# A hybrid decoder step on one core: the delta rule's triangular inverse with its small block products split into shorter groups

## The chip, the cores and the metric

One core of a Trainium2 chip. The metric is the device time of one execution in microseconds. The matrix engine is PE in the profile (PEld is its weight load), VectorE is DVE, ScalarE is ACT, GpSimd is POOL, SyncE is SP.

## The reference

The kernel computes one inference step of a two-layer decoder trunk for a prompt of 1024 tokens and 8 samples of one token. Layer 0 mixes retention and sparse attention, layer 1 is a gated DeltaNet with 8 heads of width 128; each has a squared-ReLU MLP. What the change touches is the delta rule of layer 1, computed in chunks:

```python
m = jnp.where(strict, jnp.einsum('nbhid,nbhjd->nbhij', kb, kc) * gam, 0.0)
eye = jnp.eye(chunk, dtype=f32)
t_inv = lax.linalg.triangular_solve(eye + m, jnp.broadcast_to(eye, m.shape), left_side=True, lower=True)
u = jnp.einsum('nbhij,nbhje->nbhie', t_inv, vc * bc[..., None])
w = jnp.einsum('nbhij,nbhjd->nbhid', t_inv, kb * jnp.exp(gc)[..., None])
```

## The kernel before

Layer 1 (`odd`, from L1632) goes head by head. The kernel uses chunks of 128, so each of the 8 heads has 8 chunks, and for each a triangular matrix of 128 x 128 is inverted. `inverse_blocks` (L2022) inverts the 16 x 16 blocks on the vector engine; `inverse_rest` (L2055) puts them together with small products on the matrix engine, for all 8 chunks of a head at once: 32 x 32 blocks from 16 x 16 ones (L2065, two sets of 32 products), 64 x 64 blocks from 32 x 32 ones (L2083, L2093, L2096), 128 x 128 from 64 x 64 (L2106, L2111). The products address a 32 x 32 or 64 x 64 part of the array.

All this is woven into the dense projections. `mm3` (L181) does three matmuls per k-step and then calls `tick` (L232), which takes one step of one of two lanes in turn; when the lane whose turn it is has nothing left, the other is taken. A step is what a generator does up to its next `yield`. Lane 0 holds `head(h)` (decays, products of keys and queries, `inverse_blocks`), lane 1 holds `chain(h - 1)`: first `inverse_rest`, then the recurrence over the 8 chunks (L1840 to L1871), then the output norm and its transposes (L1833). A head's three projections are 72 k-steps. `chain` takes 34 turns, `head` 14, and `head` does not begin `inverse_blocks` until the chain of the previous head has finished `inverse_rest` (the flag `inv`, which both share tiles for). After the last head the gate projections (L1916 on, 24 k-steps for each of 8 heads) go on with the last two chains in lane 1 and the samples in lane 0; at head 6 of these, what is left of the last chain is drawn in one go (L1915).

The order in which an engine gets its instructions is set at build time by a planner: it goes by the order in the program, raised priorities, and what it reckons to be ready. All PSUM tiles of the lanes (`iv`, `tn`, `m`, `t2`) come from one ring of four banks.

Of the kernel before, what the change touches and what calls it, by code (L numbers as in the profile page):

```python
# [20 lines left out]
OP = mybir.AluOpType  # L21
# [112 lines left out]
class _Step:  # L134
# [1920 lines left out]
    def inverse_rest(self, N, U, Up, Tp, NM, Pt, Pt2, TT):  # L2055

        nc = self.nc
        V = nc.vector
        f = lambda y: y.rearrange("p a b -> p (a b)")
        ps = [self.side('iv'), self.side('iv')]  # L2060
        for p, l, r in ((ps[0], NM, Tp), (ps[1], Pt, Up)):
            for q in range(4):
                x = slice(32 * q, 32 * q + 32)
                for c in range(8):
                    nc.tensor.matmul(p[x, 32 * c:32 * c + 32], l[x, c], r[x, c], start=True, stop=True)  # L2065
            if p is ps[0]:
                nc.scalar.copy(f(Pt), p[:, 0:256])
                yield
        V.tensor_tensor(f(Up), f(Up), ps[1][:, 0:256], op=OP.subtract)
        V.transpose(f(Tp), f(Up))  # L2070
        for q in range(2):
            x = slice(32 * q, 32 * q + 32)
            nc.scalar.copy(TT[x, :, x], Tp[x])
        for q in range(3, -1, -1):
            x = slice(32 * q, 32 * q + 32)
            nc.gpsimd.tensor_copy(U[x, :, x], Up[x])
        yield
        p = self.side('iv')
        v32 = lambda y: y[:, 0:256].rearrange("p (c m) -> p c m", c=8)
        for i in (0, 2):  # L2080
            x, y = slice(32 * i, 32 * i + 32), slice(32 * i + 32, 32 * i + 64)
            for c in range(8):
                nc.tensor.matmul(p[y, 32 * c:32 * c + 32], N[x, c, y], Tp[x, c], start=True, stop=True)  # L2083
        for i in (0, 2):
            y = slice(32 * i + 32, 32 * i + 64)
            with self.tc.high_priority(offset=100):
                nc.scalar.copy(Pt[y], v32(p)[y])
        yield
        p = self.side('iv')
        for i in (0, 2):  # L2090
            x, y = slice(32 * i, 32 * i + 32), slice(32 * i + 32, 32 * i + 64)
            for c in range(8):
                nc.tensor.matmul(p[x, 32 * c:32 * c + 32], Pt[y, c], Up[y, c], start=True, stop=True)  # L2093
        x, y = slice(0, 32), slice(32, 64)
        for c in range(8):
            nc.tensor.matmul(p[y, 32 * c:32 * c + 32], Up[y, c], Pt[y, c], start=True, stop=True)  # L2096
        for i in (0, 2):
            x, y = slice(32 * i, 32 * i + 32), slice(32 * i + 32, 32 * i + 64)
            nc.scalar.mul(U[x, :, y], v32(p)[x], -1.0)
        nc.scalar.mul(TT[32:64, :, 0:32], v32(p)[32:64], -1.0)  # L2100
        yield
        p = self.side('iv')
        lo, hi = slice(0, 64), slice(64, 128)
        v64 = lambda y: y.rearrange("p (c m) -> p c m", c=8)
        for c in range(8):
            nc.tensor.matmul(p[hi, 64 * c:64 * c + 64], N[lo, c, hi], TT[:, c], start=True, stop=True)  # L2106
        nc.scalar.copy(Pt2[hi], v64(p)[hi])
        yield
        p = self.side('iv')
        for c in range(8):  # L2110
            nc.tensor.matmul(p[lo, 64 * c:64 * c + 64], Pt2[hi, c], U[hi, c, hi], start=True, stop=True)  # L2111
        nc.scalar.mul(U[lo, :, hi], v64(p)[lo], -1.0)
        yield
# [117 lines left out]
```

## Time and profile before

| | us |
|---|---|
| timed runs: 2976.19, 2978.12, 2978.9; median | 2978.12 |
| profiled execution | 2991.83 |
| its span, first to last instruction | 2990.2 |
| PE busy in the span | 2878.2 (96%) |
| DVE busy | 1966.3 (66%) |
| ACT busy | 1245.8 (42%) |
| POOL busy | 240.8 (8%) |
| mean granted PE clock | 0.981 |

The steps below are read from the profiled execution, which took 13.7 us longer than the median of the timed runs. A granted clock of 1.00 is 2.4 GHz, 0.50 is 1.2 GHz. PE is the engine to watch: it is busy nearly all the time, though a busy PE can still run at the lower clock.

### The profile page before, as it was taken

The page shows a single profiled execution, that of the slowest core. Times are in us where ns is not written, and L with a number is a line of the kernel's source. Part 1 is how long each engine was busy: PE and PEld are TensorE (multiplying, and loading weights), DVE is VectorE, ACT ScalarE, POOL GpSimd, SP SyncE. Part 2 cuts the span into 40 slices and gives each one's busy share as a digit, 9 for nine tenths or more (in the row PEclk, how much of TensorE's full clock was granted, in tenths as well). Part 3 has the DMA queues.
Part 4 walks back from the last instruction along what each step waited for, and adds up shares of the span by engine and source line. Part 5 has one row for each costly group of instructions (what it writes and reads, how often), then busy time and mean ns, then how long its engine had stood idle before and what let it go on. Part 6 is the DMA issues. An engine that isn't in the chain of part 4 may idle for free. (4 is left out here: it accounts for less than half of the span.)

```text
span 2990.2 us, 57153 instructions
## 1 busy us (share of the span) xinstructions
PE 2878.2 (96%) x22980; PEld 2684.1 (90%) x22980; DVE 1966.3 (66%) x5147; ACT 1245.8 (42%) x2498; POOL 240.8 (8%) x328
## 2 busy tenths in 40 slices
PE   8999999999899999999999999999999999999997
PEld 6559997799799999999988999999998999999997
DVE  4569897448755765454677766764768657765557
ACT  4457734426733431111364565542348434321111
POOL 0210002100000000000001111111100000000002
PEclk9989998999999999999999999998999999999998
DMA  8665325213433556552221222223524426343222
GB/s 277 189 201 142 86 72 177 78 50 106 155 121 128 194 168 191 170 164 94 62 83 40 65 62 49 60 77 113 170 82 129 158 96 205 124 141 106 72 71 65
DMA packets 282678, 358.50 MB, mean 120 GB/s; under 512 B 49494, under 2 KB 230523, under 8 KB 281644
## 3 DMA queue, kind: packets, MB, share of 16 engines
q1 hardware_dynamic: 258786, 272.86, 30.3%
q0 software_dynamic: 23296, 81.85, 8.4%
q8 instruction: 180, 2.95, 0.4%
q14 instruction: 86, 0.70, 0.1%
q10 hardware_dynamic: 330, 0.13, 0.0%
HBM read 271.45 MB, written 80.12 MB: 118 GB/s over the span
## 5 line engine op out<-in xcount | busy, mean ns | idle before, releaser
L188 PE MATMUL bank<-XH,whi 128*128 128x256 f32 (+4 forms) x3488 | 906.3, 305 | 1.9 <-ACT N L1268 0.8
L188 PE MATMUL bank<-XH,wlo 128*128 128x384 f32 (+5 forms) x2720 | 825.5, 304 | 0.9 <-DVE wlo L177 0.9
L188 PE MATMUL bank<-XL,whi 128*128 128x256 f32 (+5 forms) x2976 | 792.6, 302 | 2.2 <-DVE XL L426 1.9
L188 PEld LDWEIGHTS bank<-XH,whi 128*128 128x128 f32 (+1 forms) x3488 | 604.2, 188 | 24.2 <-issue 11.1
L188 PEld LDWEIGHTS bank<-XL,whi 128*128 128x128 f32 (+1 forms) x2976 | 525.7, 188 | 17.8 <-issue 9.5
L188 PEld LDWEIGHTS bank<-XH,wlo 128*128 128x128 f32 (+2 forms) x2720 | 511.7, 188 | 7.8 <-issue 5.0
L638 DVE SCALAR_TENSOR_TENSOR N<-bank,G,N 128x256 f32<-128x256 f32 x576 | 274.8, 481 | 312.6 <-PE bank L188 311.5
L176 ACT CAST whi<-raw 128x1024 fp32r<-128x1024 f32 x142 | 147.5, 1039 | 443.2 <-PE bank L188 397.8
L188 PE MATMUL bank<-W,whi 128*128 128x260 f32 (+1 forms) x1152 | 207.7, 282 | 2.9 <-DVE accS L646 1.5
L177 DVE TENSOR_TENSOR wlo<-raw,whi 128x1024 fp32r<-128x1024 f32 x142 | 173.2, 1220 | 45.6 <-ACT whi L176 44.8
L704 PE MATMUL bank<-W,whi 128*128 128x256 f32 x1094 | 182.9, 284 | 12.4 <-ACT whi L697 7.3
L704 PE MATMUL bank<-W,wlo 128*128 128x256 f32 x1082 | 182.0, 284 | 9.5 <-ACT wlo L697 4.2
L704 PE MATMUL bank<-XH,whi 128*128 128x260 f32 x896 | 181.2, 285 | 8.1 <-ACT N L719 3.0
L704 PE MATMUL bank<-XH,wlo 128*128 128x260 f32 x896 | 181.2, 285 | 4.4 <-DVE wlo L691 3.0
L188 PEld LDWEIGHTS bank<-W,whi 128*128 128x128 f32 x1152 | 176.0, 188 | 8.3 <-DVE N L638 2.5
L697 ACT CAST whi<-raw 128x512 fp32r<-128x512 f32 x168 | 103.9, 622 | 170.9 <-PE bank L704 60.3
L704 PEld LDWEIGHTS bank<-W,whi 128*128 128x128 f32 x1094 | 155.0, 188 | 18.8 <-ACT whi L697 9.5
L704 PEld LDWEIGHTS bank<-W,wlo 128*128 128x128 f32 x1082 | 154.5, 188 | 14.6 <-ACT wlo L697 5.7
L188 PE MATMUL bank<-W,wlo 128*128 128x256 f32 (+1 forms) x576 | 162.0, 283 | 0.5 <-DVE wlo L177 0.5
L691 DVE TENSOR_TENSOR whi<-raw,whi 128x512 fp32r<-128x512 f32 x168 | 115.1, 688 | 67.4 <-ACT whi L697 63.6
L697 ACT CAST wlo<-raw 128x512 fp32r<-128x512 f32 x168 | 103.3, 621 | 133.8 <-PE bank L704 50.4
L691 DVE TENSOR_TENSOR wlo<-raw,wlo 128x512 fp32r<-128x512 f32 x168 | 114.6, 687 | 63.0 <-ACT wlo L697 60.5
(628 smaller groups left out, 5461.0 us busy)
## 6 DMA issues: line engine op xcount, KB each, us to landing
raw<-in_mlp_up_dram SPq DMA_DIRECT2D x96, 512.0 KB, 4.2
N<-in_ada_w_dram SPq DMA_DIRECT2D x80, 512.0 KB, 5.3
W<-hD SPq DMA_DIRECT2D x64, 516.0 KB, 4.4
raw<-in_mlp_down_dram SPq DMA_DIRECT2D x60, 512.0 KB, 3.5
hD<-N POOLq DMA_DIRECT2D x32, 520.0 KB, 4.0
N<-resD SPq DMA_DIRECT2D x32, 512.0 KB, 4.6
hD<-N POOLq DMA_DIRECT2D x32, 512.0 KB, 3.6
raw<-in_odd_w_in_dram SPq DMA_DIRECT2D x32, 512.0 KB, 4.2
```

What stands on the lines that cost most here:

```text
L176: nc.scalar.copy(hi[:, :k * m], raw[:, :k * m])
L177: nc.vector.tensor_tensor(lo[:, :k * m], raw[:, :k * m], hi[:, :k * m], op=OP.subtract)
L188: self.nc.tensor.matmul(out, ww[:, i, ms], xx[:, c0:c1], start=start and i == 0 and j == 0, stop=stop and i == nk - 1 and j == 2)
L638: nc.vector.scalar_tensor_tensor(r, ps[:, :256], g[:, dt, 0:1], r, op0=OP.mult, op1=OP.add)
L691: sub = lambda o, x, y: V.tensor_tensor(o, x, y, op=OP.subtract)
L697: nc.scalar.copy(hi, a)
L704: nc.tensor.matmul(o, ww[:, k], xx, start=start and k == 0 and n == 0, stop=k == 3 and n == 2, skip_group_check=True)
```

## The change

Each set of products in `inverse_rest` is interrupted by a `yield` once part of it is issued: after two of the four strips of 32 partitions in L2065's two sets (16 products, then 16), after the first of the two blocks in L2083's set (8, then 8), and after the first of the blocks in L2093's set (8, then 8 with the 8 of L2096 behind them). The second PSUM tile of L2065's sets is taken when its set begins, not with the first. No operation is added or removed.

```diff
-        ps = [self.side('iv'), self.side('iv')]
-        for p, l, r in ((ps[0], NM, Tp), (ps[1], Pt, Up)):
+        for l, r in ((NM, Tp), (Pt, Up)):
+            p = self.side('iv')
             for q in range(4):
                 x = slice(32 * q, 32 * q + 32)
                 for c in range(8):
                     nc.tensor.matmul(p[x, 32 * c:32 * c + 32], l[x, c], r[x, c], start=True, stop=True)
-            if p is ps[0]:
+                if q == 1:
+                    yield
+            if l is NM:
                 nc.scalar.copy(f(Pt), p[:, 0:256])
                 yield
-        V.tensor_tensor(f(Up), f(Up), ps[1][:, 0:256], op=OP.subtract)
+        V.tensor_tensor(f(Up), f(Up), p[:, 0:256], op=OP.subtract)
...
                 nc.tensor.matmul(p[y, 32 * c:32 * c + 32], N[x, c, y], Tp[x, c], start=True, stop=True)
+            if i == 0:
+                yield
...
                 nc.tensor.matmul(p[x, 32 * c:32 * c + 32], Pt[y, c], Up[y, c], start=True, stop=True)
+            if i == 0:
+                yield
```

## Rows read from the trace of the kernel before

**Rows 1.** The page, section 1: busy us, share of the span, instructions.
```profile
PE 2878.2 (96%) x22980; PEld 2684.1 (90%) x22980; DVE 1966.3 (66%) x5147; ACT 1245.8 (42%) x2498; POOL 240.8 (8%) x328
```
**Rows 2.** Windows: stretch, length, busy us by engine, PE clock, DMA share, GB/s.
```profile
core 0: us, PE busy (x) PEld busy (x) DVE busy (x) ACT busy (x) POOL busy (x), PEclk, DMA share, GB/s
1600.00:2060.00 460.00, 452.32 (x4409) 421.24 (x4408) 298.03 (x1087) 240.00 (x635) 76.25 (x92) 0.96 0.26 68
1609.00:1612.45 3.45, 3.45 (x22) 3.29 (x20) 2.68 (x4) 1.31 (x3) 2.13 (x3) 0.51 0.34 84
1720.00:1740.00 20.00, 20.00 (x317) 18.66 (x317) 11.31 (x28) 13.07 (x33) 4.05 (x5) 1.00 0.18 55
1970.80:1981.10 10.30, 10.30 (x122) 9.54 (x118) 5.30 (x7) 4.72 (x15) 2.42 (x4) 0.50 0.13 52
2034.80:2039.10 4.30, 4.30 (x126) 4.08 (x125) 0.00 (x0) 1.06 (x2) 0.54 (x1) 1.00 0.32 126
2039.10:2059.60 20.50, 20.50 (x152) 18.39 (x151) 3.06 (x6) 5.99 (x13) 4.84 (x7) 0.50 0.41 129
```
**Rows 3.** The product lines, all heads: count, ns min/median/max, first and last start.
```profile
L2065 PE MATMUL bank<-N x1024: 191/191/258, 1604.8 to 2039.0; 32*32 32x32 f32 x171
L2083 PE MATMUL bank<-N,N x256: 191/191/258, 1614.3 to 2042.8; 32*32 32x32 f32 x128
L2093 PE MATMUL bank<-N x256: 191/191/258, 1616.3 to 2046.4; 32*32 32x32 f32 x128
L2096 PE MATMUL bank<-N x128: 191/191/257, 1617.1 to 2047.0; 32*32 32x32 f32 x128
```
**Rows 4.** Timeline of PE (start, us, line, count): a group of 64.
```profile
1719.74 0.33 PE L188 MATMUL bank<-XH,wlo 128*128 128x384 f32 x1
1720.00 1.91 PE L2065 MATMUL bank<-N 32*32 32x32 f32 x64
1721.84 0.44 PE L188 MATMUL bank<-XH,whi 128*128 128x384 f32 x1
1722.12 0.34 PE L188 MATMUL bank<-XL,whi 128*128 128x384 f32 x1
```
**Rows 5.** The same: a group of 32.
```profile
1728.72 0.34 PE L188 MATMUL bank<-XH,wlo 128*128 128x384 f32 x1
1728.99 1.09 PE L2083 MATMUL bank<-N,N 32*32 32x32 f32 x32
1730.01 0.45 PE L188 MATMUL bank<-XH,whi 128*128 128x384 f32 x1
1730.30 0.34 PE L188 MATMUL bank<-XL,whi 128*128 128x384 f32 x1
```
**Rows 6.** The same: a group of 48.
```profile
1731.52 0.33 PE L188 MATMUL bank<-XH,wlo 128*128 128x384 f32 x1
1731.78 1.00 PE L2093 MATMUL bank<-N 32*32 32x32 f32 x29
...
1732.71 0.57 PE L2096 MATMUL bank<-N 32*32 32x32 f32 x13
1733.21 0.44 PE L188 MATMUL bank<-XH,whi 128*128 128x384 f32 x1
1733.49 0.34 PE L188 MATMUL bank<-XL,whi 128*128 128x384 f32 x1
```
**Rows 7.** Timeline of PE ahead of the seventh head's inverse; in brackets idle time before.
```profile
1968.94 0.66 PE L1833 MATMUL bank<-cst,N 128*128 128x128 f32 x4 [1.53 <-DVE N L1827]
...
1969.88 0.81 PE L2065 MATMUL bank<-N 32*32 32x32 f32 x23
```
**Rows 8.** L2053 in two heads, and the second head's first products.
```profile
L2053 DVE STREAM_TRANSPOSE N<-N x2: 436/436/437, 1654.1 to 1711.4; 128x256 f32<-128x256 f32 x2
...
1655.62 0.62 PE L2065 MATMUL bank<-N 32*32 32x32 f32 x14
```
**Rows 9.** Waits of PE, 1600 to 2060: total us, times, longest.
```profile
PE bank L1833 <- DVE N L1827: 4.3, 6, 1.5
```
**Rows 10.** Timeline of PE in the gate projections: the last transposes.
```profile
2120.91 0.60 PE L1833 MATMUL bank<-cst,N 128*128 128x128 f32 x4
```

## The prediction

> **What bounds the kernel now.** I read the page's busy shares first, then the stage in which the change lies, then single groups of products, and last the waits. The matrix engine is busy 96% of the span [rows 1]. In the stretch that holds the eight inverses it is busy 452.32 of 460 us, at a mean granted clock of 0.96 [rows 2]. So the matrix engine sets this stage's end, and the rest of the inverse (copies, vector transposes) runs beside it. What is put on that engine, or what its clock gives back, comes out at the end nearly one for one.
>
> The reader is to see two things in the stage. First, the clock. In three stretches it is granted at 0.50 (1.2 GHz instead of 2.4): 3.45 us in the first head's inverse, 10.30 us in the seventh's, 20.50 us in the eighth's, together 34.25 us [rows 2]. In the other five inverses it stayed at 1.00, as in the third head's stretch [rows 2]. Before the longest fall the engine was not idle: 4.30 of 4.30 us busy, with 126 matmul records, all but a few of them 32x32 products [rows 2]. Second, the products themselves. Per head L2065 has 128 instructions in two runs of 64, L2083 has 32, and L2093 with L2096 has 48 (each product is two instructions) [rows 3].
>
> **What a group of products costs.** One group's whole cost is read from the dense matmuls around it: from the start of the last one before the group to the start of the second one after it, less two ordinary slots. A slot is 1.22/7 = 0.174 us (the seven steps from 1730.30 to 1731.52) [rows 5, 6]. The group of 64: 1722.12 - 1719.74 - 0.35 = 2.03 us [rows 4]. The group of 32: 1730.30 - 1728.72 - 0.35 = 1.23 us [rows 5]. The group of 48: 1733.49 - 1731.52 - 0.35 = 1.62 us [rows 6]. The three lie on a line: 16 instructions more cost 0.40 us, and 0.42 us is left that does not depend on the number. It is spent at the two edges, where the array goes from full tiles to 32x32 tiles and back: the first dense matmul after a group holds its successor for 0.28 us instead of 0.174.
>
> **The change part by part.** Removed: nothing. All products, copies and subtractions stay. Added: four yields per head, which split the two runs of 64 into 32 + 32 each, the run of 32 into 16 + 16 and the run of 48 into 16 + 32. That is 4 x 8 = 32 more groups. Between the halves one turn of the other lane and two k-steps of dense matmuls (six of them) are emitted, so the edges are paid again: 32 x 0.41 = **+13.1 us**. The ends of this price: 0 if the planner runs the halves together again, 0.42 each (13.4) if not. I take nearly the full price, since dense matmuls are ready at once and stand earlier in the program than the second half, and since the three group sizes agree on it. The 64x64 products (L2106, L2111) are not touched.
>
> What it can give back is the clock. 34.25 us at half clock are at most 17.1 us of lost work [rows 2]. Shorter product groups with dense work between them speak for fewer falls. But not all three are in reach: ahead of the seventh head's fall the engine waited 1.53 us for the vector engine, and the products had begun at 1969.88, under a microsecond before the clock fell at about 1970.8 [rows 2, 7]. A group of half the length would have looked the same to that point. Without its 5.1 us, 12 us are left. And the profiled execution took 2991.83 us, the median of the timed runs is 2978.12 us, 13.7 less: nothing says that the timed runs hold as much low clock as the profiled one. Bounds 0 and 17.1; I take the middle, **-8.6 us**.
>
> Moved: the chain of a head needs 38 turns instead of 34, and the next head, which waits for the end of that inverse, 18 instead of 14. One head's projections give 72 turns, so both still end in time; the four extra turns cost eight k-steps, 24 x 0.174 = 4.2 us of delay, which the 16 spare turns cover. Three places have less cover:
> - The second head's transpose of its block inverse (L2053) ended at 1654.1 + 0.44, and the products that read it began at 1655.62: 1.1 us to spare; for the third head it is 8.2 us (1711.4 + 0.44 against 1720.00) [rows 4, 8]. With 4.2 us of delay the former is late by up to 3.1 us, and the dense matmuls queued behind it on the matrix engine wait with it, if the planner does not place it later. 0 to 3.1, I take 1.
> - The transposes L1833 of a finished head wait for the vector engine's L1827, 4.3 us in six cases, the longest 1.5 [rows 9]. They come 4.2 us later, to other neighbours. Between -4.3 (all gone) and +4.3 (doubled); the place shifts, the causes stay: 0.
> - In the last stage lane 1 has 72 turns before the gate projection of head 6, and two chains need 76 (68 before). The last four are then drawn together, the final L1833 (now at 2120.91 [rows 10]) included, and its store and reload come some 16 k-steps later; the DMA queues of GpSimd and SyncE are passed by nothing else. From 0 to the longest such wait, 1.5; I take 1.
>
> Sum: +13.1 - 8.6 + 1 + 0 + 1 = **+6.5 us**. Against the profiled execution's own 2991.83 us (its span 2990.2 and 1.6 around it) that is 2998.3; against the median, **2984.6 us**, 0.22% slower.
>
> **A rule weighed.** The longest fall came with the matrix engine busy in every part of the 4.30 us before it [rows 2]. The Trainium skill, "TensorE: Matmul & The Clock Gate", section "Why this matters for your kernels", tells the reader to avoid idle gaps between bursts so that the clock does not drop. The trace disagrees as far as that idle is meant as the cause: here the busy share was 1.00 and the granted clock fell to 0.50.
>
> **The rivals.**
> - Full recovery. All three stretches come back to 1.00 and the timed runs have them too: 13.1 + 2 - 17.1 = -2.0, 2976.1 us, no change that can be told. For it: in five of eight inverses the clock held even with the long groups. Against it: the wait before the seventh head's fall remains [rows 7].
> - Faster. The mechanism is the same, but the timed runs hold more low clock than the profiled one, because other inverses fall in them. It decides when more than 21 us are given back (13.1 + 2 + 6), which is 42 us at half clock against the 34.25 seen. With five of eight inverses at the mean of the three seen (11.4 us), 57 us are low and 28.5 come back: 2978.1 + 15.1 - 28.5 = 2964.7. Against it: the timed runs end sooner than the profiled one and lie within 2.7 us of each other.
> - Nothing recovered. The falls do not come from the products but from waits before them, as in the seventh head [rows 7]; then only the price is left: +13.1 + 2, 2993.2 us. This is what the page's rule above would make of the change, too. Against it: the eighth head, with no wait at all in the 4.30 us before its fall [rows 2].
> - The change does not do what it says. The planner, which orders each engine's instructions, joins the halves again; neither price nor gain, only the moved turns: 2978 to 2980. Against it: dense work is always ready in this stage.
>
> **How the numbers follow.** This kernel's measurement tells about 0.2%, or 6 us, from no change. Forecast (price paid, part of the clock back): 0.43, of which 0.32 ends above +6 us and 0.11 below. Full recovery 0.24, faster 0.15, nothing recovered 0.10, halves joined 0.08. So slower 0.32 + 0.10 = 0.42, same 0.11 + 0.24 + 0.08 = 0.43 less 0.01 for full recovery with a smaller price, which goes to faster: 0.42 and 0.16. Slower and same weigh alike; the single likeliest case is the forecast, whose own range is 2979 (12 us back) to 2990 (3 us back). The range has to take in full recovery and nothing recovered with its waits: 2970 to 2995; the deeper faster cases and the worst waits are left out.
>
> **What would show it.** L2065 with four runs of 32 per head instead of two of 64, L2083 with two of 16, dense matmuls between all of them, each group of 32 still at about 1.2 us by the same reckoning; 32 groups more. In the windows, low-clock stretches in the inverses that add up to well under 34 us, with the seventh head's case still possible wherever L1833 waits just ahead of products. L1833's waits near 4 us in sum. The forecast is wrong if the split group costs clearly less than 0.4 us more, if the timed runs gain over 20 us, or if a new wait above 3 us stands ahead of L2065 in the second head or ahead of the gate projections of heads 6 and 7.

## The result, and the profile after

| us | before | after |
|---|---|---|
| timed runs beside each other, median of six each | 2977.15 (2970.32 to 2979.43) | 2997.93 (2989.1 to 3007.16) |
| ratio, 95% interval | | 1.0070 [1.0052, 1.0088] |
| profiled execution | 2991.83 | 2995.84 |
| its span | 2990.2 | 2994.2 |
| mean granted PE clock | 0.981 | 0.987 |

The change costs 20.8 us (0.0052 to 0.0088 of 2977, so 15.5 to 26.2), where 6.5 were forecast; the time lies 3 us above the end of the range. Slower was one of the two likeliest signs, but the size is three times the forecast.

The page of after, section 1 (busy us, share, instructions), answers to [rows 1]: the instruction counts are the same and the span is longer. In this pair the matrix engine is even a little less busy, but its busy time contains what ran at half clock: four more executions of before, reported below, had 2865.2 to 2871.3 us. So the pages alone don't say what was added.

```profile
PE 2875.6 (96%) x22980; PEld 2677.5 (89%) x22980; DVE 1983.1 (66%) x5147; ACT 1249.9 (42%) x2498; POOL 234.1 (8%) x328
```

Windows of after (stretch, length, busy us by engine, PE clock, DMA share, GB/s) answer to [rows 2]. First the stretch of the inverses, then the eighth head's inverse, then three stretches at or just behind places in which the clock still falls.

```profile
core 0: us, PE busy (x) PEld busy (x) DVE busy (x) ACT busy (x) POOL busy (x), PEclk, DMA share, GB/s
1600.00:2060.00 460.00, 444.02 (x4232) 404.50 (x4231) 306.99 (x1067) 239.27 (x629) 68.09 (x91) 1.00 0.25 64
2026.00:2060.00 34.00, 33.39 (x376) 30.51 (x376) 11.19 (x34) 10.94 (x28) 6.99 (x12) 1.00 0.47 146
1975.00:1980.00 5.00, 5.00 (x80) 4.32 (x80) 3.94 (x6) 3.23 (x8) 0.06 (x1) 0.95 0.45 139
2125.00:2140.00 15.00, 14.80 (x78) 13.89 (x78) 8.36 (x34) 7.71 (x21) 2.03 (x3) 0.77 0.44 141
2145.00:2155.00 10.00, 7.79 (x38) 7.08 (x39) 9.21 (x34) 0.18 (x2) 0.89 (x1) 0.66 0.50 142
```

The reader is to see two things in the first two rows. The clock is 1.00 where it was 0.96, and in the eighth head, where 20.50 us ran at 0.50, it never falls. And the engine is busy 444.02 of 460 us instead of 452.32: 8.3 us of idle time more in the same stretch.

The products of after, on the matrix engine's timeline (start, us, line, count): a split half of 32, and one of 16.

```profile
1713.04 0.60 PE L1742 MATMUL bank<-cst,W 128*128 128x128 f32 x4
1713.39 0.42 PE L188 MATMUL bank<-XH,whi 128*128 128x384 f32 x1
1713.65 0.33 PE L188 MATMUL bank<-XL,whi 128*128 128x384 f32 x1
1713.83 0.34 PE L188 MATMUL bank<-XH,wlo 128*128 128x384 f32 x1
1714.09 1.09 PE L2065 MATMUL bank<-N 32*32 32x32 f32 x32
1715.12 0.45 PE L188 MATMUL bank<-XH,whi 128*128 128x384 f32 x1
1715.40 0.34 PE L188 MATMUL bank<-XL,whi 128*128 128x384 f32 x1
...
1725.68 0.34 PE L188 MATMUL bank<-XH,wlo 128*128 128x384 f32 x1
1725.95 0.69 PE L2097 MATMUL bank<-N 32*32 32x32 f32 x16
1726.56 0.45 PE L188 MATMUL bank<-XH,whi 128*128 128x384 f32 x1
1726.85 0.34 PE L188 MATMUL bank<-XL,whi 128*128 128x384 f32 x1
```

By the reckoning of [rows 4 to 6] the half of 32 costs 1715.40 - 1713.83 - 0.35 = 1.22 us and the group of 16 costs 1726.85 - 1725.68 - 0.35 = 0.82. With 1.23, 1.62 and 2.03 of before they lie on one line, 0.40 us for 16 instructions and 0.42 for a visit. The price of a break was right.

**An account of the stage.** To compare executions I cut out the stage by three marks: the first L1742 transposes of the layer (a), the first 128x256 matmul of the output projection (b), and the first L638, which takes that projection's result (the join is from b to it). The change touches only what lies between a and L638. Low clock is summed over windows of 5 us from a to b as twice (1 - granted clock) times length, so half of it is lost. Here are the windows a to b of before, of one more execution of before (the lowest clock of five), and of after.

```profile
1544.60:2143.06 598.46, 586.43 (x5318) 550.61 (x5317) 414.73 (x1517) 306.78 (x805) 96.82 (x117) 0.97 0.29 78
```
```profile
1535.14:2137.26 602.12, 589.38 (x5319) 553.20 (x5318) 415.38 (x1517) 306.86 (x805) 96.90 (x117) 0.96 0.29 78
```
```profile
1532.25:2142.94 610.69, 591.19 (x5317) 545.52 (x5315) 425.88 (x1495) 310.14 (x805) 88.37 (x115) 0.99 0.28 76
```

| us | before, mean of five executions | after, mean of two | difference |
|---|---|---|---|
| a to first L638 | 604.9 (603.1 to 607.7) | 623.6 (623.1, 624.0) | +18.7 |
| groups of 32x32 products | 34 | 61 | 27 x 0.41 = +11.1 |
| at half clock, a to b | 36.2 (30.8 to 44.4) | 11.9 (10.2, 13.6) | -24.3, half of it: -12.2 |
| PE idle, a to b | 13.0 (12.0 to 13.7) | 19.7 (19.5, 19.8) | +6.7 |
| join | 6.0 (5.6 to 6.7) | 13.5 (13.4, 13.6) | +7.4 |
| not in these rows (18.7 less the four) | | | +5.7 |

So 18.7 us stand in this stage. From L638 to the end after takes 3.1 us less (838.9 against 842.0, means), which leaves 15.6 us from a to the end, the low end of the timed interval. Of the last 5.7 us of busy time a part is that dense matmuls are interrupted more often by other work too: 390 stretches of them against 328, of which 27 are the groups, and the first dense matmul after L1742's transposes holds its successor for 1713.65 - 1713.39 = 0.26 us instead of 0.174; 35 such places at 0.086 are 3.0 us, an estimate. Some 3 us remain without a place.

**The idle time.** Waits of the matrix engine, 1560 to 2080 (total us, times, longest): first before, then after.

```profile
PE bank L1833 <- DVE N L1827: 4.3, 6, 1.5
PE bank L1850 <- DVE N L1846: 2.7, 6, 1.1
...
PE bank L1843 <- DVE N L1865: 0.3, 1, 0.3
```
```profile
PE bank L1850 <- DVE N L1846: 6.2, 7, 1.2
PE bank L1833 <- DVE N L1827: 5.1, 5, 3.3
PE bank L1843 <- DVE N L1865: 3.0, 6, 1.0
...
PE bank L2112 <- ACT N L2106: 1.6, 6, 0.5
```

L1850 and L1843 are the recurrence over the chunks, which follows the inverse in lane 1 and so runs four turns later than before. One of the new waits, on the timeline of the vector engine and then of the matrix engine:

```profile
1808.18 3.08 DVE L1695 SCALAR_TENSOR_TENSOR W<-W,cwT,W 128x1056 f32<-128x1056 f32 x1
1811.20 0.66 DVE L1793 TENSOR_TENSOR N<-bank,ri 128x512 f32<-128x512 f32 x1
...
1815.18 0.34 DVE L1846 SCALAR_TENSOR_TENSOR N<-bank,M,N 128x128 f32<-128x128 f32 x1
```
```profile
1815.58 0.49 PE L1850 MATMUL bank<-N,N 128*128 128x128 f32 x2 [0.89 <-DVE N L1846]
```

L1695 is the convolution and L1793 and L2043 are the next head's work; the recurrence's L1846 stands in their queue, and L1850 waits for it.

**The join.** Windows b to the first L638, before and after.

```profile
2143.06:2148.66 5.60, 5.60 (x47) 5.40 (x46) 4.89 (x16) 2.38 (x6) 0.00 (x0) 1.00 0.89 282
```
```profile
2142.94:2156.30 13.36, 10.20 (x56) 9.00 (x55) 12.29 (x43) 2.46 (x6) 1.78 (x2) 0.74 0.44 127
```

The vector engine is busy 12.29 of 13.36 us: it still works on the samples. Their state updates (L2185, L2191 in after), from the groups by line: first and last start stand behind the durations.

```profile
L2185 DVE SCALAR_TENSOR_TENSOR N<-N,N,bank x64: 336/343/349, 2078.3 to 2139.6; 128x128 f32<-128x128 f32 x64
```
```profile
L2191 DVE SCALAR_TENSOR_TENSOR N<-N,N,bank x64: 336/342/351, 2080.7 to 2148.0; 128x128 f32<-128x128 f32 x64
```

The last update starts 3.5 us before the output projection in before and 5.1 us after its start in after. The matrix engine waits 13.36 - 10.20 = 3.16 us in the join. Two of the samples' own products (L1285) now stand between the projection's matmuls there and wait for the vector engine, and so does the projection's next matmul (total us, times, longest):

```profile
PE bank L1285 <- DVE rsi L265: 1.8, 1, 1.8
PE bank L188 <- DVE XL L1935: 0.8, 1, 0.8
PE bank L1285 <- DVE rsi L264: 0.5, 1, 0.5
```

The mean clock of 0.74 puts 6.9 us of the join at half clock, 3.5 us lost. So the +7.4 of the join are some 3.1 us of waiting, 3.5 us of clock and under 1 us of other work, and the 11.9 us at half clock in the table leave this fall out.

### The profile page after: what moved, and what is told of

It is laid out like the page before. It is cut to its first block, busy times and chain, and to the rows that moved or that the text cites. A ratio compares the mean times of both kernels' runs of the same rounds, so it can differ in the third digit from the quotient of the medians.

```text
span 2994.2 us, 57171 instructions
## 1 busy us (share of the span) xinstructions
PE 2875.6 (96%) x22980; PEld 2677.5 (89%) x22980; DVE 1983.1 (66%) x5147; ACT 1249.9 (42%) x2498; POOL 234.1 (8%) x328
## 5 line engine op out<-in xcount | busy, mean ns | idle before, releaser
L188 PEld LDWEIGHTS bank<-XH,whi 128*128 128x128 f32 (+1 forms) x3488 | 604.5, 188 | 24.8 <-issue 11.1
L638 DVE SCALAR_TENSOR_TENSOR N<-bank,G,N 128x256 f32<-128x256 f32 x576 | 274.9, 481 | 313.9 <-PE bank L188 313.5
L704 PEld LDWEIGHTS bank<-W,whi 128*128 128x128 f32 x1094 | 154.9, 188 | 17.2 <-ACT whi L697 7.7
```

Of the source, the lines that this page charges most:

```text
L188: self.nc.tensor.matmul(out, ww[:, i, ms], xx[:, c0:c1], start=start and i == 0 and j == 0, stop=stop and i == nk - 1 and j == 2)
L638: nc.vector.scalar_tensor_tensor(r, ps[:, :256], g[:, dt, 0:1], r, op0=OP.mult, op1=OP.add)
L704: nc.tensor.matmul(o, ww[:, k], xx, start=start and k == 0 and n == 0, stop=k == 3 and n == 2, skip_group_check=True)
```

## The experiments

The fences that follow hold the windows a to b of the kernel named, as above.

**Turns only.** The four yields, in places where no group is split, so that the turns are moved without the edges (one more execution was profiled beside another of after).

```diff
         for l, r in ((NM, Tp), (Pt, Up)):
             p = self.side('iv')
+            yield
...
+        yield
         for i in (0, 2):   # ahead of L2083's and of L2093's products
```

> The four added yields per head stand ahead of the groups instead of inside them: no group is split, but the chain still needs 38 turns and the next head and the samples start as late as in the changed kernel. Theory T (turns: the delay of the chain and of the samples costs by waits in the recurrence, 7.5 us more idle time of PE in the stage, and 7.7 us at the join to the output projection): 2988 to 2995, nearly all of the loss. Theory P (price: 27 more groups at 0.41 us, which the clock gives back only in part): within 3 us of the kernel before, 2975 to 2980.

> The turns without the splits, a second look. D: low clock in the stage 8 to 20 us again, PE idle some 23 us. S: the 10.2 us of the first look were chance; 25 to 40 us now.

> The changed kernel, a second look: low clock 10 to 25 us in the stage, PE idle 19 to 20 us, the time from the stage's first transposes to the first add of the output projection 621 to 627 us, against 603 to 608 us in five looks of before. If the first look was an odd one, these differ by more than 5 us.

Measured: 2987.16 us, 1.0033 [1.0012, 1.0054], +9.8 us; the further execution 3011.71, and after's 3004.7, whose account came out as expected (623.1 us, 10.2 low). Theory P is out. Theory T is nearer, but its range begins at 2988, and it is about half of the loss, not nearly all: the other 11.0 us come with the splits, near the price of 27 groups, though both ratios have intervals of 5 to 6 us either way. Windows a to b, first execution, then the further one:

```profile
1532.24:2133.20 600.96, 577.93 (x5316) 539.95 (x5315) 425.35 (x1495) 309.98 (x805) 86.68 (x115) 0.99 0.29 77
```
```profile
1548.84:2156.83 607.99, 587.49 (x5316) 548.85 (x5315) 425.64 (x1495) 309.88 (x805) 86.29 (x115) 0.97 0.28 77
```

With 33 groups the idle time is 23.0 and 20.5 us, the join 13.6 and 13.4. Both delay terms of after (idle and join) are here in full without a split, at 7.3 to 10.1 us each above before. So is the rest that stands in no row: 5.4 and 4.7 us by the same reckoning. It comes with the turns, not with the splits. The clock came back in the first execution (10.2 us low) without shorter groups; in the second, 30.6 us are low, in other places (around the first head's inverse, at 1985, 2090 and from 2138 on). One kernel's stage thus varies by 20 us of low clock; from a to L638 it took 614.5 and 621.3 us. Most of the 24 us between the two executions lies ahead of a (1532.24 and 1548.84), which no edit touches.

**Splitting some heads.** The yields only in heads 0 to 5, or only in heads 6 and 7 (counted from 0).

```diff
-                if q == 1:
+                if q == 1 and split:   # split = h < 6, or h >= 6
```

> Groups are split in the first six chains only; the last two, which run beside the gate projections, are as before. T: the join to the output projection is as before (first L638 some 5 us after the projection starts, not 13), so 8 of the 20.8 us go and 2983 to 2988 are left, with the waits in the recurrence. P: three quarters of the price stay, 2990 to 2994.

> The counterpart: groups are split in the last two chains only. T: the loss at the join to the output projection is there, the waits in the recurrence of heads 0 to 5 are not: 2984 to 2990. P: 8 more groups, 3.3 us, less what the clock gives back in the last two heads: 2973 to 2981.

Measured: 3000.1 us, 1.0068 [1.0041, 1.0095], and 2989.49, 1.0031 [1.0013, 1.0048]. The two do not add up to the whole (20 + 9 against 21), though within their intervals of about 8 and 5 us either way they may. With heads 0 to 5 split, both theories missed (2988 and 2994 were their upper ends); with heads 6 and 7 split, T's range holds. What the two do tell apart is the two delay terms and the clock. Idle time from a to b is 20.0 us with heads 0 to 5 split and 14.7 with heads 6 and 7 (13.0 in before, 19.7 in after): it comes mostly with the turns of the first six heads. The later taking of L2065's second PSUM tile is in every head of both kernels, so it does not make this difference. Windows of the kernel with heads 0 to 5 split, before and in the fall at its unsplit eighth inverse, and of the one with heads 6 and 7 split, at the unsplit first and over both split ones:

```profile
2041.00:2046.00 5.00, 5.00 (x125) 4.76 (x120) 0.63 (x2) 0.94 (x2) 0.66 (x2) 0.87 0.29 111
2046.00:2064.00 18.00, 18.00 (x143) 15.88 (x142) 2.43 (x5) 5.62 (x12) 4.72 (x7) 0.50 0.48 147
```
```profile
1595.00:1616.00 21.00, 21.00 (x219) 19.04 (x216) 5.75 (x10) 7.40 (x17) 2.74 (x5) 0.54 0.22 50
1950.00:2050.00 100.00, 93.48 (x959) 86.08 (x958) 54.88 (x187) 42.45 (x114) 16.33 (x25) 1.00 0.36 102
```

In these stretches the clock falls to 0.50 where the groups are left long, and holds where they are split. It is not so in every head: the third to the sixth hold with long groups, in before too. The join is 5.7 us where the seventh and eighth heads are not split and 12.9 where they are; which of the two it follows was not separated.

**The edges without the turns.** A 128x128 transpose into an unused part of the bank, at each of the 32 places of a split, in the kernel before.

```diff
+                if q == 1:
+                    nc.tensor.transpose(p[:, 256:384], self.ident, self.ident)
...
+            if i == 0:   # in L2083's and in L2093's set
+                nc.tensor.transpose(p[:, 256:384], self.ident, self.ident)
```

> The kernel before with one 128x128 transpose of the identity into unused columns at each of the 32 places where the change splits a group: the edges are paid, no turn is added, no dense work comes in between. The extra transposes are work that the kernel does not need, about 0.1 us each. Price theory (each split costs its edges, 0.41 us, whatever else happens): 13 + 3 = 16 us slower, 2990 to 2997, with the join to the output projection as before (5 to 6 us). Rival (the edges cost little by themselves and the loss of the changed kernel is waits and delay): 3 to 6 us slower, 2979 to 2984.

Measured: 3004.48 us (four runs), 1.0097 [1.0064, 1.0130]. Its windows a to b, and on the timeline of the matrix engine a run of 64 broken in two:

```profile
1538.98:2151.34 612.36, 601.23 (x5351) 559.62 (x5349) 414.80 (x1517) 307.58 (x805) 96.82 (x117) 0.97 0.28 77
```
```profile
1718.60 0.34 PE L188 MATMUL bank<-XH,wlo 128*128 128x384 f32 x1
1718.87 1.09 PE L2065 MATMUL bank<-N 32*32 32x32 f32 x32
1719.89 0.33 PE L2067 MATMUL bank<-cst 128*128 128x128 f32 x1
1720.15 1.09 PE L2065 MATMUL bank<-N 32*32 32x32 f32 x32
1721.18 0.44 PE L188 MATMUL bank<-XH,whi 128*128 128x384 f32 x1
1721.46 0.34 PE L188 MATMUL bank<-XL,whi 128*128 128x384 f32 x1
```

The broken run costs 1721.46 - 1718.60 - 0.35 = 2.51 us, 0.48 more than 2.03 unbroken; 32 x 0.48 = 15.4. The trace's stage grew by 13.6 (to 618.5) with idle time (11.1) and join (6.1) near those of before, so the price of an edge stands by itself. The timed runs grew by 19 to 39 us against 2971.46 for before beside them, more than that and more than the price theory's 2997; the rest has no place in the trace. The low clock stayed at 37.6 us, with 28 us at 0.51 in the eighth inverse: groups half as long, with one transpose between them, do not hold the clock. The Trainium skill, "TensorEngine Tiling (Array Packing)", section "Key Properties", says that a change of tiling mode drains the engine; the rows fit that, and put both edges together at about 0.4 us.

**The four empty turns.** `chain` has four turns ahead of its last transposes in which nothing is done. They were taken out of after, and out of before.

```diff
             nc.gpsimd.dma_start(a['ssm_prompt'][0, 0, h], S)
-            for _ in range(4):
-                yield
             turned(1)
```

> The changed kernel without the four empty turns ahead of the last transposes (L1874): 34 turns per chain again, with all groups split. T: the last chain ends by itself again and the samples start 8 k-steps later instead of 16, so about half of the loss goes, 2984 to 2990. P: no change against the changed kernel, 2995 to 3001.

> The kernel before without the four empty turns ahead of the last transposes: 30 turns per chain, chains and samples of the last stage end earlier. If late turns are what costs at the join, and before still pays for some of that, it gains: join below 5.6 us, 2968 to 2975. If before has cover enough, no change: 2974 to 2981.

Measured: after without them 2995.91, 1.0053 [1.0033, 1.0073]; before without them 2975.74, 1.0004 [0.9988, 1.0021], no change. For after, T's 2984 to 2990 missed. There the edit gives back the count of turns, and yet idle time stays at 19.0 us and the join at 11.1. So the idle time does not go by the number of a chain's turns alone; within a chain the recurrence, which comes before those turns, still lies four turns later behind its start. Why the join stayed long was not followed further.

The profiled execution of before without the empty turns took 2967.27 us, with 17.1 us at half clock from a to b and a join of 3.0. Its eighth inverse, which starts at 2015.0, holds the full clock with long groups:

```profile
2010.00:2040.00 30.00, 30.00 (x379) 28.07 (x378) 14.51 (x63) 11.60 (x30) 6.96 (x12) 1.00 0.60 194
```

So in this one execution neither shorter groups nor added turns were needed for the clock to hold in that inverse. What else moved beside it was not followed.

**The samples later in lane 0.** They wait from their first turn on for the eighth head's inverse (the loop at L1901). Here they are put into the lane only when that is done.

```diff
             x['inv'] = True
+            if h == 7:
+                self.lanes[0].append(smp)
...
-        self.lanes[0].append(samples())
-        smp = self.lanes[0][-1]
+        smp = samples()
```

> The changed kernel, but the samples enter lane 0 only when the last inverse is done, so that waiting for it takes no turns from the two chains in the gate projections. Nothing else moves. Theory T (lost turns in the gate projections cost 7.8 us at the join to the output projection): join at 3 to 6 us instead of 13.4, 2986 to 2993. Price theory: the join is not what costs, 2995 to 3001.

> The same edit on the kernel before: 66 turns of lane 1 are no longer halved by an idle lane 0. T: the join falls from 5.6 to 3 us or less, as without the empty turns, 1 to 3 us faster, within what can be told. Risk: the two recurrences then have only one k-step between their turns and wait for VectorE, some us slower.

Measured: after with it 2999.65, 1.0073 [1.0052, 1.0094]; before with it 2984.58, 1.0027 [1.0009, 1.0045]. The join falls to 3.1 us in both, which was my theory of its cause, and the time does not follow: after stays at +0.7%, and before gets 8.0 us slower, where 1 to 3 us faster was expected (the risk named beside it was some us slower). Windows a to b of the former:

```profile
1534.92:2153.04 618.12, 597.88 (x5319) 550.69 (x5318) 437.37 (x1533) 309.84 (x805) 90.02 (x117) 0.98 0.29 79
```

From a to b it takes 8.0 us more than after (610.1), 6.0 of them by 23.9 us at half clock instead of 11.9. So the join's gain of 10.4 was lost again ahead of it, and from a to L638 only 2.4 are left. My theory that the join can be had by itself fell: where it was shorter, the stage was longer, and whether by the moved work or by the chance of the clock stays open.

**Distance without splitting.** Empty yields between the long groups only in heads 0, 6 and 7, no group split, and the four empty turns dropped.

```diff
+            if apart and l is Pt:   # apart = h in (0, 6, 7)
+                yield
...
+        if apart:   # ahead of L2083's and of L2093's products
+            yield
```

> Nothing split: three empty turns set the product groups further apart, only in the heads whose inverse held low clock in every look (first, seventh, eighth), and the four empty turns ahead of the last transposes are dropped, so that no chain gets longer than it was. If distance between the groups alone gives the clock back (theory D), low clock in the stage falls from 31 to 44 us to 10 to 25, idle time of PE stays at 12 to 14 us, 2968 to 2976, 4 to 10 us faster than before. If the clock needs the shorter groups (theory S), low clock stays at 30 to 40 us: within 4 us of before.

```profile
1535.54:2127.72 592.18, 574.95 (x5319) 539.90 (x5317) 420.85 (x1519) 307.62 (x805) 91.19 (x117) 0.99 0.30 80
```

Measured: 2976.53, 0.9989 [0.9971, 1.0008], 3.3 us less than before beside it. Low clock is 10.3 us, idle time 17.2, join 5.2; from a to L638 it takes 597.3, 7.6 less than before. The clock is as theory D had it, the idle time is not, and the median lies above D's range and within S's 4 us of before. By this one trace it is the better kernel; the timed runs don't settle it.

**The kernel before against itself.** It was timed as if it were a change, and profiled again, to see how far executions of one kernel differ.

> The kernel before once more, for a second look at the granted clock and the idle time of PE in the stage. In the first look 37.6 us of the 598.5 us stage were at 0.50, and the stretch ahead of the stage was some 10 us longer than in the changed kernel and the first four experiments. Theory L (the timed runs of before hold less low clock than that look, so the change gave back less than it seemed): 10 to 25 us low, stage 585 to 592 us. Rival (the look was typical): 33 to 42 us low, stage 595 to 600 us.

> The same again. L: 10 to 25 us low, stage 585 to 592 us; rival: 33 to 42 us low, 595 to 600 us.

> The kernel before against itself, in rounds: the ratio shows what such a comparison can tell, and gives one more look. Theory L (executions of before differ in how much low clock the last inverses hold; the looks taken so far, 30.8 to 44.4 us low in the stage, are high ones): ratio 1.000 within 0.002, and if the look taken is a fast execution (below 2978 us) it shows under 25 us low in the stage. Rival (every execution holds 30 to 44 us): also a look below 2978 us shows 30 or more, and the 10 us lie elsewhere.

> One more look of before. L: the low clock in the stage goes with the time, some 0.5 us of time for each us of low clock, 15 us low at about 2972, 40 us low at about 2985. Rival: no such relation.

Measured: 1.0006 [0.9990, 1.0021]; single executions took 2985.01, 2985.35, 2982.2 and 2982.05 us. With the first (2991.83) these are the five of the account: 30.8 to 44.4 us at half clock, mostly in the seventh and eighth inverses each time. For these five theory L fell. But none came out below 2978 us, and each took longer than the median of the timed runs beside it (2971.46 to 2979.83): what a shorter execution of before holds was not seen.

## Why the prediction was wrong, by its own steps

**What bounds the stage: right.** The matrix engine is busy 591.19 of 610.69 us in after, and what was put on it came out at the end.

**The price of a group: right.** 1.22 us for a half of 32, and 0.82 for one of 16; the edges alone cost it again in the kernel with transposes. There were 27 more groups, not 32: 11.1 us instead of 13.1. Not every head had two runs of 64, as the prediction read it: in the second head (the 14 products of [rows 8]) and in the eighth (10) the first run was broken already in before. And in the first head of after three of the four splits are joined.

**The clock: right in kind.** From a to b the profiled executions gave back 12.2 us instead of 8.6; less the 3.5 that the fall in the join costs, it is 8.7. That this is close to the forecast is luck: the 8.6 was the middle of two bounds, and the join's fall was not foreseen. Whether the timed runs of before hold as much low clock stays open, since each of the five took longer than the median beside it. The 13.7 us by which the first of them exceeds the median are no sign of it: its stage, 604.1 us, is an ordinary one, and it lost the time ahead of a (1544.60, against 1530.83 to 1537.70 in the four others). That the seventh head could not be reached was half right: L1833 waits there again, 3.25 us, and the clock falls as that wait ends, but it is back before the first product (0.95 from 1975 to 1980).

```profile
1972.34 1.11 PE L1833 MATMUL bank<-cst,N 128*128 128x128 f32 x4 [3.25 <-DVE N L1827]
```

**The moved turns: the step that failed.** The prediction said that "the four extra turns cost eight k-steps, 24 x 0.174 = 4.2 us of delay, which the 16 spare turns cover", and the three places with less cover came to 1 + 0 + 1. In their place stand 6.7 us of idle time and 7.4 us of join, 14.1 us.
- The spare turns do cover the end of a chain; no wait ahead of the next head's L2065 appeared on the matrix engine. What they don't cover is where the recurrence lies against the vector engine's queue. The prediction looked for late ends and asked of L1833 alone what its new neighbours are; it did not ask it of L1850 and L1843, which have eight chunks in each head.
- L1833 itself went from 4.3 to 5.1, inside its bounds. The wait at the second head's L2053, priced at 1, did not appear.
- The last stage was walked in lane 1 only, with at most 1.5 us. Lane 0 holds the samples, and they wait for the same inverse. They come out 8.6 us later against the output projection, on a vector engine that has its copies and residuals to do there. That the last two heads cause this is shown (join 5.7 and 12.9); that it goes through the samples is argued from the waits of L1285 and from the join's fall to 3.1 when the samples are queued late. What the join is worth by itself is not shown, since the time did not follow when it was shortened.

**Not in the sum at all:** 5.7 us of busy time, in part the dense work's more frequent interruptions. It recurs with the turns alone, so it too belongs to the moved turns.

By these rows the sum is 11.1 - 12.2 + 6.7 + 7.4 + 5.7 = 18.7, where the 5.7 is what the others leave over; 20.8 were timed. The forecast put +2 where 14.1 stand: these 12.1 are most of the 14.3 by which it missed.

**The rivals.** "Nothing recovered" gave the nearest time (2993.2) by a false mechanism: half clock fell from 36 to 12 us, or to 19 with the join. Nor were the halves joined, but for the first head, and full recovery and faster fall with the delay terms.

**What stays open:** some 3 us of busy time in after; how the timed runs of both kernels spread over more or less low clock (after 2989 to 3007 us), and so what the clock gave back in them; what the join is worth; whether setting the groups apart without splits, or dropping the empty turns of before, makes a faster kernel.

## What to carry to other kernels

A yield put into a woven lane moves all that follows it: walk every lane and each later step that reads another engine, and ask at each what will stand ahead of it in that engine's queue, not only whether the lane still ends in time. A group of small-tile products costs its two edges each time it is visited, so try distance between groups before you make them shorter; that this gains time was not shown here. A gain in clock can be real and still be spent on waits in the same stage.

## What the runs showed of the hardware

The clock fell to 1.2 GHz with the matrix engine fully busy: in the unsplit eighth inverse 18.00 of 18.00 us at 0.50, after 5.00 of 5.00 busy. Groups half as long with a single transpose between them fell there too (28 us at 0.51). Long ones held it there with added turns between them (both executions of turns only, and distance), and also in before without its empty turns. Elsewhere in the stage falls remained (10.2, 30.6, 10.3 and 17.1 us low in these four). The Trainium skill, "TensorE: Matmul & The Clock Gate", section "Why this matters for your kernels", tells the reader to avoid idle gaps between bursts. The eighth inverse's fall does not agree with that, nor does after's fall between 2125 and 2140 (0.77, with 14.80 of 15.00 us busy). After's falls at L1833's 3.25 us and in the join do. The seventh inverse's falls in before can be read either way: L1833 had waited ahead of that inverse in all five executions, 1.5 us in the first [rows 7] and 1.8 to 2.1 in the others.
